# Second FFN of a decoder layer: products of mixed quads grouped by kind, five of eight quads mixed

## The chip, the cores and the metric

The kernel runs on one core of a Trainium2 chip. The metric is the device time of one execution in microseconds, as a median over runs. The engines that matter here are TensorE (PE in the profile; PEld is its weight loads), VectorE (DVE), ScalarE (ACT), and the queues of SyncE (SP) and GpSimd (POOL), which issue DMAs.

## The reference

One decoder layer over 272 positions (16 meta tokens and 256 of the sequence), model width 2048, all in fp32:

```
h += 0.5 * SwiGLU_1(RMSNorm(h))                 # 2048 -> 5632 -> 2048
z  = RMSNorm(h) @ W_in                          # q, k, v, indexer, conv, gates
h += W_out(sigmoid(ga) * attn(z) + sigmoid(gc) * conv(z))
h += 0.5 * SwiGLU_2(RMSNorm(h))                 # the second FFN
swiglu(x) = (silu(x @ w_gate) * (x @ w_up)) @ w_down
```

The change concerns the last line but one, the second FFN, where only the 256 positions of the output are computed: two halves of 128 tokens.

## The kernel before

**Products.** TensorE is fed with operands of the type fp32r. Every fp32 operand is split into a high part (ScalarE's copy to fp32r, `whi<-raw`, L175) and a low part (VectorE's subtraction, `wlo<-raw,whi`, L176). One product of a 128x128 block of tokens with a 128x512 block of weights is then three matmuls (`trio`, L407 to 410): high by high, high by low, low by high.

**The weight stream.** The class `Stream` brings in all weights in the order of use. A load is 1 MB at most (four weight blocks of 128x512), in one of four raw tiles (`raw` and `raws`), and SyncE's queue issues it. A *unit* is what one split makes ready, one or two blocks; its high and low parts lie in one of four pairs of buffers. Before TensorE's work of unit k is issued, the split of unit k+3 is (`AHEAD = 3`), so that it takes the buffers of unit k-1. The order on each engine is the order in which the program writes the instructions: `st.put(fn, slot)` puts a piece of other work `slot // 2` units on, an even slot before the split made there, an odd one behind it. The table `LAG` holds these slots.

**The second FFN.** It has two groups of 6 and 5 middle blocks of 512. A group has one *up stage* for each middle block f (gate and up together, 16 weight blocks deep), and then two *down parts* (d = 0 and d = 2), each for two groups of 512 output columns. Work in an up stage goes by *quads*: two weight blocks of depth (k) by two groups of 512 columns (gate and up), against two halves of tokens. An up stage has 8 quads, a down part 12 (first group) or 10 (second).

- A *plain* quad is 8 products on 4 weight blocks: two units of two blocks and four products.
- A *mixed* quad is Strassen-Winograd: 7 products P1 to P7. P1, P2 and P3 use the quad's own weight blocks, P4 to P7 sums of them. The sums of weights are made earlier by *jobs* (`job`, L554): a load of 1 MB on POOL's queue, four VectorE operations (L568, `made<-made`), and a store to scratch in DRAM. The sums of the inputs (`combos`) are five small VectorE operations (L702 to 706) and splits (ScalarE L688, VectorE L689).

Before, four of eight quads (1, 3, 5 and 6) are mixed in an up stage (one in the first), and 4, 4, 3 and 5 in the down parts: 57 in all. The units of a mixed quad, A, B, C and D, stand where the quad stands in the order, between plain ones (`order`, L89). P1, P5, P6 and P7 of all the mixed quads of a stage add up in banks of their own, and after the last mixed quad `spread` (L764) brings them together: one ScalarE copy (L767) and three VectorE adds (L768 to 770).

**At the end of an up stage** `gather` adds these sums to the other banks (VectorE L780 to 782, `few<-three,u`, `u<-one,u`, `u<-two,u`), two `silu` follow on ScalarE (L788), the product with up on VectorE (`times`, L794), then the transposition through DRAM (L637 and POOL's DMAs) and the split of the middle block (L812, L813). The last middle block of a group is turned on VectorE instead (sixteen transposes, L513), then split (ScalarE L464, VectorE L465, `mid<-mt`), since the down part reads it soon.

Of the jobs, 46 are done in the first FFN and 11 beside the output projection, before the second.

## Time and profile before

| what | value |
|---|---|
| median of 3 runs | 2109.67 us (2109.22 to 2110.75) |
| span of the profiled execution | 2106.9 us |
| PE, DVE, ACT busy | 2098.8, 1582.4, 1058.9 us |
| moved by DMA | 575.64 MB, mean 273 GB/s |
| second FFN in the profile | from about 1420 us to the end |

The profiled execution is one whose span is 2106.9 us; the median of the runs is 2.8 us above this span. A row of a timeline begins with its start and its length in us; a row of groups ends with busy us, mean ns of one, and the idle time before it with what ended it. A row "ACT whi L175 <- DVE wlo L176: 5.4, 5, 1.7" says who waited, for whom, how long in total, how often and the longest. Mean durations overlap a little from one VectorE instruction to the next, so that the distance of their starts (the pitch) is what counts in a sum.

### The profile page before, as it was taken

Reading aid. Unit: us, or ns where it says so; the run is one execution under the profiler, and the core shown is the slowest. Engines: PE = TensorE matmul, PEld = TensorE weight load, DVE = VectorE, ACT = ScalarE, POOL = GpSimd, SP = SyncE. Lnnn points to the kernel's source line nnn. Section 1 sums busy time; section 2 is a strip of 40 time slices with the busy share of each in tenths; the row PEclk is TensorE's granted clock in tenths of the full one; section 3 lists DMA queues with packets and bytes.
Section 4 is the critical chain, followed back from the end, with each engine's and each line's share of the span. In section 5 each row is a group of like instructions: output and inputs, shape, how many; then the busy total and the mean of one; then the engine's idle time right before and its main releaser. Section 6 shows DMA issues by size and latency. Waiting matters only on the chain.

```text
span 2106.9 us, 31863 instructions
## 1 busy us (share of the span) xinstructions
PE 2098.8 (100%) x12731; PEld 1889.9 (90%) x12731; DVE 1582.4 (75%) x2144; ACT 1058.9 (50%) x1342; POOL 106.0 (5%) x207
## 2 busy tenths in 40 slices
PE   9999999999999999999999999999999999999998
PEld 9999999999999999889988888888888888888887
DVE  7676766676776766578679678769788896878897
ACT  6444433344444445565444444456575565566654
POOL 0000000000000000000000000011000000000000
PEclk9999999999999999999999999999999999999999
DMA  7788888888888865445468886667988777799865
GB/s 265 260 320 327 324 315 322 311 337 310 322 313 325 328 224 177 164 159 181 152 216 329 323 301 223 219 233 255 314 314 300 281 268 247 282 306 319 306 250 207
DMA packets 85908, 575.64 MB, mean 273 GB/s; under 512 B 10112, under 2 KB 10880, under 8 KB 23808
## 3 DMA queue, kind: packets, MB, share of 16 engines
q1 hardware_dynamic: 64080, 438.34, 58.4%
q0 software_dynamic: 21104, 134.23, 17.1%
q8 instruction: 99, 1.62, 0.3%
q10 hardware_dynamic: 576, 1.05, 0.1%
q14 instruction: 49, 0.40, 0.1%
HBM read 504.90 MB, written 68.68 MB: 272 GB/s over the span
## 4 chain that ended last, share of the span: by engine, by line
PE 98%; DVE 1%; DMA 1%; issue 0%; ACT 0%; DVEq 0%; ACTq 0%
PE three L409 5%; PE three L408 5%; PE three L410 5%; PE pd L375 4%; PE pd L376 4%; PE pd L374 4%; PE pu L374 4%; PE pg L375 4%; PE pg L374 4%; PE pu L375 4%; PE pg L376 4%; PE pu L376 4%; PE pgt L402 3%; PE pgt L404 3%; PE pgt L403 3%; PE one L408 3%
## 5 line engine op out<-in xcount | busy, mean ns | idle before, releaser
L176 DVE TENSOR_TENSOR wlo<-raw,whi 128x1024 fp32r<-128x1024 f32 (+1 forms) x771 | 906.2, 1188 | 464.5 <-ACT whi L175 457.7
L175 ACT ACTIVATE whi<-raw 128x1024 fp32r<-128x1024 f32 (+1 forms) x771 | 786.4, 1030 | 883.4 <-PE pd L375 146.2
L375 PE MATMUL pd<-mid,whi 128*128 128x272 f32 x704 | 201.9, 287 | 0.0
L376 PE MATMUL pd<-mid,wlo 128*128 128x272 f32 x704 | 201.9, 287 | 0.0
L374 PE MATMUL pd<-mid,whi 128*128 128x272 f32 x704 | 201.9, 287 | 0.0
L374 PE MATMUL pu<-act,whi 128*128 128x272 f32 x672 | 192.8, 287 | 0.0
L376 PE MATMUL pu<-act,wlo 128*128 128x272 f32 x672 | 192.7, 287 | 0.0
L376 PE MATMUL pg<-act,wlo 128*128 128x272 f32 x672 | 192.7, 287 | 0.0
L375 PE MATMUL pg<-act,whi 128*128 128x272 f32 x672 | 192.7, 287 | 0.0
L375 PE MATMUL pu<-act,whi 128*128 128x272 f32 x672 | 192.7, 287 | 0.0
L374 PE MATMUL pg<-act,whi 128*128 128x272 f32 x672 | 192.7, 287 | 0.0
L568 DVE TENSOR_TENSOR made<-made 128x512 f32<-128x512 f32 x228 | 156.3, 685 | 0.0
L408 PE MATMUL three<-whi,act 128*128 128x512 f32 x352 | 137.2, 390 | 0.1
L409 PE MATMUL three<-wlo,act 128*128 128x512 f32 x352 | 137.0, 389 | 0.0
L410 PE MATMUL three<-whi,act 128*128 128x512 f32 x352 | 137.0, 389 | 0.0
L376 PEld LDWEIGHTS pd<-mid,wlo 128*128 128x128 f32 x704 | 132.7, 188 | 0.0
L374 PEld LDWEIGHTS pd<-mid,whi 128*128 128x128 f32 x704 | 132.7, 188 | 0.0
L375 PEld LDWEIGHTS pd<-mid,whi 128*128 128x128 f32 x704 | 132.7, 188 | 0.0
L176 DVE TENSOR_TENSOR wlo<-raws,whi 128x1024 fp32r<-128x1024 f32 x92 | 103.5, 1140 | 31.7 <-ACT whi L175 31.0
L374 PEld LDWEIGHTS pu<-act,whi 128*128 128x128 f32 x672 | 126.7, 188 | 0.0
L374 PEld LDWEIGHTS pg<-act,whi 128*128 128x128 f32 x672 | 126.7, 188 | 0.0
L376 PEld LDWEIGHTS pg<-act,wlo 128*128 128x128 f32 x672 | 126.6, 188 | 0.0
(381 smaller groups left out, 4482.7 us busy)
## 6 DMA issues: line engine op xcount, KB each, us to landing
raw<-in_wgu_dram SPq DMA_DIRECT2D x123, 1024.0 KB, 6.4
raw<-in_wd_dram SPq DMA_DIRECT2D x63, 1024.0 KB, 6.7
made<-in_wgu_dram POOLq DMA_DIRECT2D x41, 1024.0 KB, 10.6
made<-made POOLq DMA_DIRECT2D x41, 1024.0 KB, 6.5
raw<-made SPq DMA_DIRECT2D x31, 1024.0 KB, 6.1
raw<-in_wcv_dram SPq DMA_DIRECT2D x24, 1024.0 KB, 4.9
raw<-in_wgc_dram SPq DMA_DIRECT2D x24, 1024.0 KB, 5.1
raw<-in_wga_dram SPq DMA_DIRECT2D x24, 1024.0 KB, 5.4
```

Source lines behind the costliest of these rows:

```text
L175: nc.scalar.activation(hi[:, :n], raw, AF.Copy)
L176: nc.vector.tensor_sub(lo[:, :n], raw, hi[:, :n].bitcast(F32))
L374: nc.tensor.matmul(ps, whi, xhi, start=first, stop=False)
L375: nc.tensor.matmul(ps, whi, xlo, start=False, stop=False)
L376: nc.tensor.matmul(ps, wlo, xhi, start=False, stop=last)
L402: nc.tensor.matmul(ps, xhi, whi, start=k + i == 0, stop=False)
L403: nc.tensor.matmul(ps, xhi, wlo, start=False, stop=False)
L404: nc.tensor.matmul(ps, xlo, whi, start=False, stop=k + i == n - 1)
L408: nc.tensor.matmul(ps, x(0), w[0], start=first, stop=False)
L409: nc.tensor.matmul(ps, x(0), w[1], start=False, stop=False)
L410: nc.tensor.matmul(ps, x(1), w[0], start=False, stop=last)
L568: getattr(nc.vector, f"tensor_{op}")(to, a, b)
```

## The change

- In the up stages but the first, five quads of eight are mixed (0 to 4); in the first, none. In each of the four down parts four are: 66 in all.
- Products of the mixed quads are grouped by kind. An up stage runs (`mixed_first`): P1 of the five quads, P2, then P6, P7, P5 and the first P4, each unit two blocks of one kind in a row (13 units of two products), P3 with the plain quads behind, the rest of P4 between them. A down part runs (`plain_first`) 14 plain units in the first group's first part, 10 in the second group's (8 and 4 in the later parts), then the kinds.
- One bank takes several kinds in turn. After the last product of a kind ScalarE copies the bank out (`copy`, `u<-single` or `u<-double`); the adds of `spread` are gone, `gather` stays.
- Other work finds new slots: `times` one unit later, `turn_gated` in the calm units 16 to 18 of the next stage, the split of the middle block two stages later (units 14 and 15). The input sums of the down part stand at units 7, 9, 11, 13, their splits at 8, 10, 12, 14; a split is ScalarE's pieces and then VectorE's in one go. In the first up stage `silu` reads the banks directly.
- Jobs: 46 in the first FFN, 8 beside keys and queries (every 4 units), 12 beside the output projection. Each store goes to a tile where a quad's four sums lie apart, in pieces of 2 KB instead of 8 KB.
- The weights of the second FFN lie in DRAM in one stream in the order of use (`w2`), and once more for the jobs (`wj`). A load is of up to four blocks that follow each other in one of the two streams (own weights, sums). An up stage with mixed quads loads 47 blocks, where it was 44.

```diff
-MIXED = 1, 3, 5, 6
-FIRST_MIXED = 5,
+MIXED = 0, 1, 2, 3, 4
+DOWN_MIXED = (4, 4), (4, 4)
+EARLY_FROM = 2
+EARLY_EVERY = 4
+EARLY = 8
-DOWN_MIXED = {6: (6, 8, 9, 10), 5: (5, 6, 7)}
 LAG = dict(
-    spread=(0, 0, 1, 1), gather=(0, 0, 0), silu=(1, 1), times=(1,), turn=(1, 1), move=4, hi=(28, 33),
-    lo=(28, 33), last_times=(1,), last_turn=(5, 5, 8, 10), last_split=12, half=(3, 3), drain=(2, 4, 3),
+    silu=(1, 1), times=(3,), last_turn=(9, 9, 11, 13), last_split=14, drain=(0, 2, 4), below=7,
...
+def mixed_first(mixed, plain):
+    own = in_twos(of_kind("P1", mixed) + of_kind("P2", mixed))
+    made = in_twos(sum((of_kind(x, mixed) for x in ("P6", "P7", "P5", "P4")), []))
+    rest = in_twos(of_kind("P3", mixed) + sum(plain_pairs(plain), []))
+    early = -(-3 * len(mixed) // 2)
+    seq = [("h", x) for x in own] + [("m", x) for x in made[:early]]
+    made = made[early:]
+    for i, x in enumerate(rest):
+        seq.append(("h", x))
+        if i >= 2 and i % 2 == 0 and made:
+            seq.append(("m", made.pop(0)))
+    return seq
+def plain_first(mixed, plain, lead):
+    pairs = plain_pairs(plain)
+    seq = [("h", x) for x in pairs[:lead]]
+    pairs = pairs[lead:]
+    seq += [("h", x) for x in in_twos(of_kind("P1", mixed) + of_kind("P2", mixed))]
+    for name in ("P6", "P7", "P5", "P4"):
+        seq += [("m", x) for x in in_twos(of_kind(name, mixed))]
+        if name in ("P6", "P7"):
+            seq.append(("h", pairs.pop(0)))
+    seq += [("h", x) for x in in_twos(of_kind("P3", mixed))]
+    return seq + [("h", x) for x in pairs]
...
+            bank, xx = dict(
+                P1=lambda: (m, of(2 * i, 1)), P2=lambda: (c[1, 0], of(2 * i + 1, 1)), P3=lambda: (c[1, 1], s(i, 3)),
+                P4=lambda: (c[2, 0], of(2 * i + 1, 2)), P5=lambda: (m, s(i, 0)), P6=lambda: (m, s(i, 1)),
+                P7=lambda: (c[2, 0] if m is c[2, 1] else m, s(i, 2)),
+            )[name]()
...
-                plan.append((unit, i == max(mixed) and name == "D"))
+            for name in blocks:
+                if name in ends:
+                    ends[name]()
...
+                def split():
+                    for hi, lo, x in to:
+                        nc.scalar.activation(hi, x, AF.Copy)
+                    for hi, lo, x in to:
+                        nc.vector.tensor_sub(lo, x, hi.bitcast(F32))
...
-            def spread(m):
-                add = nc.vector.tensor_add
-                return (
-                    lambda: nc.scalar.activation(u[:, 1], m[1], AF.Copy),
-                    lambda: add(u[:, 0], m[6], u[:, 1]),
-                    lambda: add(u[:, 2], m[7], u[:, 0]),
-                    lambda: add(ends, m[5][:, None, :].to_broadcast([P, 2, 512]), u[:, 0::2]),
-                )
+            def copy(to, bank):
+                return lambda: st.put(lambda: nc.scalar.activation(u[:, to], bank, AF.Copy), 0)
...
+                    if mixed:
+                        copies = dict(P1=copy(1, m), P6=copy(2, m), P7=copy(3, c[2, 0]), P5=copy(0, m))
+                    quads(c, m, act_part, act_of, mixed, seq, copies)
+                    if mixed:
+                        put(gather(x, c), (0, 0, 0))
+                    put(silu(None if mixed else x), LAG["silu"])
...
+                        put(times(None if mixed else c), LAG["times"])
+                        put(turn_gated(box), (1, 3), calm)
...
+        for i, (src, to) in enumerate(made[JOBS : JOBS + EARLY]):
+            job(lambda i=i: early_home(i), src, to, st.at + EARLY_FROM + i * EARLY_EVERY, EARLY_EVERY, i < 3)
...
-    st.later(lambda: nc.gpsimd.dma_start(to, box["x"]), 1, at + every + 4)
+    st.later(
+        lambda: nc.gpsimd.dma_start(to, box["x"].rearrange("p (t c) -> p t c", t=4)), 1, at + every + 4
+    )
```

How VectorE's order at the boundary of two up stages changes is shown by its queue. Before, from the adds of `spread` (L769, L770) over `gather` (L780 to 782) to `times` (L794) and on:

```order
L769 TENSOR_TENSOR u<-two,u 128x512
L770 TENSOR_TENSOR u<-three,u 128x2x512
L176 TENSOR_TENSOR wlo<-raw,whi 128x1024
L780 TENSOR_TENSOR few<-three,u 128x1024
L781 TENSOR_TENSOR u<-one,u 128x512
L782 TENSOR_TENSOR u<-two,u 128x512
L176 TENSOR_TENSOR wlo<-raw,whi 128x512
L794 TENSOR_TENSOR few<-u,few 128x1024
L637 STREAM_TRANSPOSE mt<-few 128x4x4x32 x2
L176 TENSOR_TENSOR wlo<-raw,whi 128x1024 x4
```

Now (L238 is the low part of a weight split, L875 to 877 `gather`, L892 `times`):

```order
L238 TENSOR_TENSOR wlo<-raw,whi 128x1024 x3
L875 TENSOR_TENSOR few<-double_14357,u 128x1024
L876 TENSOR_TENSOR u<-single_14354,u 128x512
L877 TENSOR_TENSOR u<-single_14355,u 128x512
L238 TENSOR_TENSOR wlo<-raw,whi 128x1024
L238 TENSOR_TENSOR wlo<-raws,whi 128x1024
L892 TENSOR_TENSOR few<-u,few 128x1024
L238 TENSOR_TENSOR wlo<-raw,whi 128x1024 x6
L238 TENSOR_TENSOR wlo<-raws,whi 128x1024 x2
```

The adds of `spread` and the transposes (L637) are gone from this place. Between `gather` and `times` there are now two splits of two blocks in place of one of one block.

ScalarE at the same place, now (L237 is the high part of a weight split, L884 `silu`, L866 the copy of a bank):

```order
L237 ACTIVATE whi<-raw 128x1024 x2
L884 ACTIVATE few<-few,rcol 128x512 x2
L237 ACTIVATE whi<-raw 128x1024 x2
L866 ACTIVATE u<-single_14353 128x512
L237 ACTIVATE whi<-raw 128x1024
```

The first copy of a bank comes two splits behind the silus.

VectorE at the start of the second group's first down part, before (L513 the transposes of the last middle block, L465 its low part, L702 to 706 and L689 the sums of the inputs):

```order
L513 STREAM_TRANSPOSE mt<-few 32x2x4x32 x4
L176 TENSOR_TENSOR wlo<-raws,whi 128x1024
L465 TENSOR_TENSOR mid<-mt,mid 128x4x256
L702 TENSOR_TENSOR few<-mid 128x512
L703 TENSOR_TENSOR few<-few 128x128
L704 TENSOR_TENSOR few<-few 128x128
L705 TENSOR_TENSOR few<-few 128x128
L706 TENSOR_TENSOR few<-few 128x128
L176 TENSOR_TENSOR wlo<-raws,whi 128x1024
L176 TENSOR_TENSOR wlo<-raw,whi 128x1024
L689 TENSOR_TENSOR mid<-few,mid 128x128
```

Now (L590 the transposes, L542 the low part, L778 to 782 and L796 the sums):

```order
L590 STREAM_TRANSPOSE mt<-few 32x2x4x32 x4
L542 TENSOR_TENSOR mid<-mt,mid 128x4x256
L778 TENSOR_TENSOR few<-mid 128x512
L779 TENSOR_TENSOR few<-few 128x128
L780 TENSOR_TENSOR few<-few 128x128
L781 TENSOR_TENSOR few<-few 128x128
L782 TENSOR_TENSOR few<-few 128x128
L238 TENSOR_TENSOR wlo<-raws,whi 128x1024
L796 TENSOR_TENSOR mid<-few,mid 128x128
L796 TENSOR_TENSOR act<-few,act 128x3x128
```

The low part of the middle block now follows the last transpose directly, without a weight split between, and one weight split, not two, stands between a quad's sums and their low parts.

More of the change, by code (lines that the diff above doesn't have):

```diff
@@ L405, in tokens, with trio @@
             k += len(blocks)
[L407 to L412 removed]
+    def trio(ps, x, w, first, last, halting):
+        for i, (a, b) in enumerate(((0, 0), (0, 1), (1, 0))):
+            nc.tensor.matmul(
+                ps, x(a), w[b], start=first and i == 0, stop=last and i == 2, skip_group_check=halting
+            )
```

470 lines of the change are left out of this document (261 added, 209 removed).

## The prediction

> **What bounds the kernel now.** I read the page first, then the chain of waits, then the waits of TensorE, then timelines. The page:
>
> ```profile
> span 2106.9 us, 31863 instructions
> ...
> PE 2098.8 (100%) x12731; PEld 1889.9 (90%) x12731; DVE 1582.4 (75%) x2144; ACT 1058.9 (50%) x1342; POOL 106.0 (5%) x207
> ...
> DVE  7676766676776766578679678769788896878897
> ...
> PE 98%; DVE 1%; DMA 1%; issue 0%; ACT 0%; DVEq 0%; ACTq 0%
> ```
>
> TensorE is busy for the whole span and holds 98% of the chain that ends last. The time therefore falls by each matmul taken out, as long as nothing else makes TensorE wait. VectorE is the fullest of the others, and fullest in the last third of its slices, the second FFN. TensorE's waits in the second FFN are these two groups, 1.4 us together:
>
> ```profile
> PE three L409 <- DVE wlo L176: 1.1, 2, 0.8
> ...
> PE three L408 <- ACT whi L175: 0.3, 1, 0.3
> ```
>
> The pitch of a matmul of the second FFN, from the first and last of 33 in TensorE's timeline:
>
> ```profile
> 1445.68 0.39 PE L409 MATMUL three<-wlo,act 128*128 128x512 f32 x1
> ...
> 1452.94 0.39 PE L408 MATMUL three<-whi,act 128*128 128x512 f32 x1
> ```
>
> That is 7.26 / 32 = 0.227 us, so 0.68 us for a product of three. The window 1545 to 1586 (below) is busy for all of its 41.00 us: the products are the floor.
>
> **What the change takes away.** 57 mixed quads become 66, each with 7 products in place of 8: 9 x 3 = 27 matmuls fewer, 27 x 0.227 = **-6.1**. The two waits above belong to an order that is gone: **-1.4**. The adds that spread the sums leave VectorE, and ScalarE's copies between kinds come in. These are off TensorE's path: five products (3.4 us) run between a kind's end and the next kind's stop, against one copy of 0.58 us (L767 below). I cost both at nothing; without that cover each copy would be worth 0.58.
>
> **What it adds: units half as long.** A unit's split is one ScalarE copy (whi) and one VectorE subtraction (wlo). There are four buffers, so the split of unit k+3 starts when unit k-1 ends and has three units to be ready. Before, a mixed up stage opens with the two units of a plain quad, four products or 2.72 us each, and the split of its unit 3 has 2.72 + 2.72 + 1.36 = 6.8 us. Now it opens with thirteen units of two products (1.36 us): 4.08 us. The price of what has to fit in, by groups from 1463 to 2000 us (the first two after them are VectorE's timeline, with its starts one behind another):
>
> ```profile
> L176 DVE TENSOR_TENSOR wlo<-raw,whi 128x1024 fp32r<-128x1024 f32 x191 | 227.5, 1220 | 57.5 <-ACT whi L175 53.1
> L175 ACT ACTIVATE whi<-raw 128x1024 fp32r<-128x1024 f32 x192 | 200.1, 1058 | 133.0 <-PE three L410 108.4 <-PE one L410 14.4 <-DVE wlo L176 3.8
> ...
> L788 ACT ACTIVATE few<-few,rcol 128x512 f32<-128x512 f32 x22 | 14.7, 717 | 9.3 <-DVE few L780 9.3
> ...
> L794 DVE TENSOR_TENSOR few<-u,few 128x1024 f32<-128x1024 f32 x11 | 13.4, 1222 | 0.0
> ...
> L767 ACT ACTIVATE u<-three 128x512 f32<-128x512 f32 x12 | 6.9, 578 | 0.0
> ```
>
> ```profile
> 1503.17 1.22 DVE L780 TENSOR_TENSOR few<-three,u 128x1024 f32<-128x1024 f32 x1
> 1504.31 0.68 DVE L781 TENSOR_TENSOR u<-one,u 128x512 f32<-128x512 f32 x1
> 1504.91 0.68 DVE L782 TENSOR_TENSOR u<-two,u 128x512 f32<-128x512 f32 x1
> ...
> 1508.59 4.59 DVE L176 TENSOR_TENSOR wlo<-raw,whi 128x1024 fp32r<-128x1024 f32 x4
> ```
>
> ```profile
> 1504.43 1.34 ACT L788 ACTIVATE few<-few,rcol 128x512 f32<-128x512 f32 x2 [0.98 <-DVE few L780]
> ```
>
> A wlo holds VectorE for 1.14 us (1503.17 to 1504.31; four in 4.59), an add of half the width 0.60, and two silus hold ScalarE 1.34. In 1.36 us VectorE does one wlo and has 0.22 to spare. Let 0 be the first matmul of a mixed up stage after a mixed one. Unit 22 of the old stage ends at -1.36, and allowing 0.2 to the engine that waits, whi(2) runs from -1.14, wlo(2) from -0.05 to 1.09. Behind it in VectorE's queue stand the three gathers: 1.09, 2.22, 2.82. wlo(3) starts at 3.42 and is written at 4.64; unit 3 starts at 4.08 and its second matmul wants it at 4.31: **0.35** of waiting, with the hand-over. ScalarE's silus wait for the first gather (2.3 to 3.65), whi(4) behind them ends at 4.7, wlo(4) runs from 4.7 and is in time; then the product of gate and up (times) at 5.84 holds VectorE until 6.98, and wlo(5) is written at 8.20. Unit 5, pushed back by 0.35, wants it at 7.15 + 0.23 = 7.38: **0.84**. After this the 0.22 per unit suffices. So 1.2 per boundary, and there are eight: **+9.6**. Bounds: 0, if the hand-overs leave just 0.3 and the queue is less strict than I read it, and 2.4 each, were both waits doubled.
>
> The boundary after the first (unmixed) stage has silu reading the banks itself, and the table load stands in front of it:
>
> ```profile
> L788 ACT ACT_TABLE_LOAD x1 | 1.3, 1283 | 0.0
> ```
>
> 1.3 + 1.34 on ScalarE delay whi(4) past its unit: by the same sums 0.4 and then 1.0, **+1.4** (0 to 2.6).
>
> **The down parts.** At the start of the second group's first part stand the last middle block's transposes, its split and the sums of the four mixed quads. Before (VectorE, then ScalarE):
>
> ```profile
> 2003.64 3.57 DVE L513 STREAM_TRANSPOSE mt<-few 32x256 f32<-32x256 f32 x8
> ...
> 2014.54 1.22 DVE L465 TENSOR_TENSOR mid<-mt,mid 128x1024 fp32r<-128x1024 f32 x1
> 2015.67 0.69 DVE L702 TENSOR_TENSOR few<-mid 128x512 f32<-128x512 f32 x1
> ...
> 2017.33 1.22 DVE L176 TENSOR_TENSOR wlo<-raws,whi 128x1024 fp32r<-128x1024 f32 x1
> ...
> 2019.60 0.29 DVE L689 TENSOR_TENSOR mid<-few,mid 128x128 fp32r<-128x128 f32 x1
> ...
> 2020.27 0.69 DVE L176 TENSOR_TENSOR wlo<-raw,whi 128x512 fp32r<-128x512 f32 x1
> ```
>
> ```profile
> 2013.40 1.06 ACT L464 ACTIVATE mid<-mt 128x1024 fp32r<-128x1024 f32 x1 [2.83 <-DVE mt L513]
> ```
>
> Sixteen transposes are 2 x 3.57 = 7.1; a quad's sums 2015.67 to 2017.33, 1.66, and their splits 2019.60 to 2020.27, 0.67: 2.33 a quad, four 9.3. In the new order the split of the middle block follows the last transpose directly, so VectorE idles while ScalarE makes its high part, 1.1, and does its 1.14. With nine wlo (units 8 to 16) of 1.14, 10.3, VectorE needs 28.9 us from the first transpose to the sums that P6 of the fourth quad reads in unit 15. TensorE's work from the same point (2.4 into unit 4: whi and wlo of unit 7) is 5 x 2.72 + 0.3 to unit 10, then five units of 1.36 and one product: 21.6 at most. The difference, **+7.3**, comes in two places: unit 8 reads the last middle block (VectorE has it at 2.4 + 7.1 + 2.3 + 1.1 + 1.2 = 14.1, unit 8 would start at 10.9), about 3, and units 14 and 15, about 4. The bounds are 3 (unit 8 alone) and 10. The first group's part has fourteen plain units ahead where this has ten, so that its block is ready long before unit 12; only the tail of the sums falls among short units: **+0.9**. The last part's opening: **+0.4**.
>
> **Jobs beside keys and queries.** Four operations of this row for each of eight jobs, at a pitch of 0.60, are 19 us of VectorE:
>
> ```profile
> L568 DVE TENSOR_TENSOR made<-made 128x512 f32<-128x512 f32 x228 | 156.3, 685 | 0.0
> ```
>
> ```profile
> 815.00:860.00 45.00, 45.00 (x223) 38.05 (x222) 28.60 (x80) 24.52 (x44) 0.53 (x2) 1.00 0.55 187
> 860.00:910.00 50.00, 50.00 (x261) 39.84 (x260) 32.09 (x60) 25.97 (x29) 0.00 (x0) 1.00 0.44 149
> 1100.00:1240.00 140.00, 140.00 (x619) 116.02 (x618) 108.78 (x141) 60.50 (x61) 9.04 (x17) 1.00 0.86 322
> 1545.00:1586.00 41.00, 41.00 (x182) 33.92 (x182) 34.49 (x37) 25.86 (x29) 2.74 (x5) 1.00 0.90 319
> 1554.00:1568.00 14.00, 14.00 (x64) 11.59 (x63) 8.66 (x10) 7.54 (x9) 2.18 (x4) 1.00 0.99 316
> 1568.00:1581.00 13.00, 13.00 (x59) 10.74 (x58) 11.91 (x13) 10.08 (x12) 0.00 (x0) 1.00 0.93 356
> ```
>
> (Windows: length, busy time and count of PE, PEld, DVE, ACT, POOL, then granted clock, DMA share, GB/s.) From 815 to 910 VectorE is idle for 16.4 + 17.9 = 34 us and the DMA engines about half, so the jobs fit on the average. What they push is a chain of small operations that ends on VectorE and that TensorE reads. Its slack here is 2.6 us:
>
> ```profile
> 844.03 0.18 DVE L1000 TENSOR_TENSOR zk<-rot 128x32 f32<-128x32 f32 x1
> ```
>
> ```profile
> L1098 PEld LDWEIGHTS pkt<-ident,zk x4: 138/140/140, 846.8 to 847.3; 128*128 128x128 f32 x4
> ```
>
> An operation of 0.60 per unit pushes it by one or two of them. I take **+1.0** (0 to 3).
>
> **DMA.** A mixed up stage now loads 47 blocks of 0.262 MB where it was 44, and turns 1.05 MB: 13.4 MB in 40.1 us, 333 GB/s. In its thirteen short units it is 26 blocks in 17.7 us: 385 GB/s. With the engines full (share 0.99) the trace shows 316, at 0.93 it shows 356. At 356 the stage fits (37.6 us) and the run is short by 1.4 us, most of which the loads made ahead hold (four tiles of 1 MB); at 316 the whole stage is short by 2.2. I take the first, nearer row and 0.45 for each of nine stages: **+4** (0 to 20).
>
> The Trainium skill, "DMA: Bandwidth & Descriptors", section "Where 436 GB/s comes from", gives 435 GB/s for the ports of the 16 engines and about 358 GB/s for the HBM of one core, and has the latter bind between HBM and SBUF. By the 435 the run would need 15.7 us and this term would be nothing (sum 4 lower); by the 358 it is short, as I took it, and the windows, 316 to 356 when full or nearly, agree with that one.
>
> Job stores now go in pieces of 2 KB for 8 KB. The trace has stores of such rows, and none of them is slow for its size:
>
> ```profile
> made<-made POOLq DMA_DIRECT2D x41, 1024.0 KB, 6.5
> ...
> out_dram<-first SPq DMA_DIRECT2D x2, 256.0 KB, 2.2
> ```
>
> I take nothing; the bound is rival four.
>
> **Sum.** -6.1 - 1.4 + 9.6 + 1.4 + 7.3 + 0.9 + 0.4 + 1.0 + 4 = +17.1. Span 2106.9 + 17.1 = 2124.0; the median of the runs stands 2.8 above the span (2109.67), so **2127**.
>
> **Rivals.**
> 1. *The short units hold* (faster). If VectorE's work at a boundary is 1.2 us shorter than summed, wlo(3) and wlo(5) are in time; the margins are small against 8 us of queue. For it: TensorE waits for 1.4 us in the whole second FFN now. Against it: the same rows give waits as soon as three units are 4.08 long, and the down part would have to close 7 us as well. Left are -7.5: **2102**.
> 2. *Boundaries hold, the down part doesn't* (no change): -7.5 + 7.3 + 0.9 + 0.4 + 1.0 = +2.1, **2112**.
> 3. *DMA is the bound in the up stages*: 13.4 MB at 316 need 42.3 us, 2.2 more than TensorE's 40.1 for each of nine, 20 in place of 4: **2143**. For it, the share of 0.99 in the stage before; against it, the 356.
> 4. *Stores in 2 KB pieces take twice as long*: in the first FFN, where one job comes about each 15 us and the share is like the 0.86 shown, 3 us more per job make 1.06; some 4% of 690 us, **2155**.
>
> **Chances.** Forecast 0.70, rivals 0.05, 0.10, 0.12, 0.03. The range: down to 2 (2112) because DMA at 0, half the boundary waits and the down part's lower bound take about 13 off; up to rival 3: **2111 to 2145**; the forecast's own is 2116 to 2139. A measurement of this kernel tells 0.2%, 4.2 us, from no change: faster 0.05 (rival 1), same 0.10 (rival 2), slower 0.85.
>
> **What would show it.** In the changed profile: TensorE's waits for wlo appear in pairs at each mixed stage's start, near 0.35 and 0.84, at units 3 and 5; about 3 us in unit 8 and 4 in units 14 and 15 of the second group's first down part; ScalarE's waits for raw tiles grow in the short runs, the DMA share there being near 1; matmuls 27 fewer. It would be wrong if TensorE's waits in the up stages stay under 3 us in all, or if first FFN and keys change by more than 3.

## The result, and the profile after

The changed kernel takes **2135.2 us** (median of 4 runs, 2134.2 to 2135.9), the kernel before, run beside it, 2110.2 (4 runs, 2109.2 to 2112.2). The ratio is **1.0122**, 95% interval 1.0108 to 1.0136: 25.0 us slower, where the prediction had +17 (2127, range 2111 to 2145). The profiled execution of the changed kernel has a span of 2133.3, 26.4 above the one before; the sums below are made against these 26.4. The page after, the same lines as shown of before:

```profile
span 2133.3 us, 31823 instructions
...
PE 2111.1 (99%) x12704; PEld 1884.9 (88%) x12704; DVE 1584.8 (74%) x2134; ACT 1087.0 (51%) x1373; POOL 128.7 (6%) x225
...
DVE  7667666676676758877688688768787787787786
...
PE 74%; issue 18%; DMA 4%; DVE 2%; ACT 1%; POOL 1%; DVEq 0%; ACTq 0%; POOLq 0%
```

27 matmuls fewer (12731 to 12704), yet TensorE is recorded busy for 12.3 us more, and its share of the chain that ends last falls from 98% to 74%. VectorE does the same work in all as before (1582.4 and 1584.8): it isn't fuller, it is asked for its results sooner. TensorE's waits in the second FFN, two groups and 1.4 us before, are now five and 14.9 us:

```profile
PE single L470 <- DVE wlo L238: 7.1, 13, 1.7
PE single L470 <- ACT mid L541: 3.6, 1, 3.6
PE double L470 <- DVE wlo L238: 2.2, 10, 0.3
PE single L470 <- ACT act L794: 1.5, 1, 1.5
PE single L470 <- DVE act L796: 0.5, 1, 0.5
```

That leaves half of the loss to be found. From here a matmul's *lateness* is its start less the start of the one before and less the pitch of 0.227 (0.22677 unrounded, which over 3000 matmuls matters). Summed over the second FFN the lateness of all matmuls is 32.6 us, and was 2.8 before; less 27 x 0.227 = 6.1 the second FFN is 23.7 us longer. The other 2.7 lie before it.

**A boundary of two up stages.** TensorE's timeline, at units 3 and 5 of the third up stage, and VectorE's at the same place (L875 is `gather`'s first addition, L892 `times`):

```profile
1510.80 0.61 PE L470 MATMUL double<-whi,act 128*128 128x512 f32 x2
1511.62 0.50 PE L470 MATMUL double<-wlo,act 128*128 128x512 f32 x1 [0.20 <-DVE wlo L238]
1511.96 0.63 PE L470 MATMUL double<-whi,act 128*128 128x512 f32 x2
...
1514.27 0.39 PE L470 MATMUL single<-whi,comb 128*128 128x512 f32 x1
1515.14 0.50 PE L470 MATMUL single<-wlo,comb 128*128 128x512 f32 x1 [0.49 <-DVE wlo L238]
```

```profile
1508.03 1.22 DVE L875 TENSOR_TENSOR few<-double,u 128x1024 f32<-128x1024 f32 x1
...
1512.74 1.22 DVE L892 TENSOR_TENSOR few<-u,few 128x1024 f32<-128x1024 f32 x1
1513.87 2.35 DVE L238 TENSOR_TENSOR wlo<-raw,whi 128x1024 fp32r<-128x1024 f32 x2
```

The stage begins at 1506.95 (fifteen matmuls of P1 before the first of P2 at 1510.35), so `gather` starts at 1.08, where the sum had 1.09. The two matmuls are late by 1511.62 - 1511.03 - 0.227 = 0.37 (the second of the pair at 1510.80 starts 0.23 behind it) and by 1515.14 - 1514.27 - 0.227 = 0.65; the latter reads the first of the low parts that start at 1513.87, behind `times`, which is done 1.14 on. After each wait the next start is 0.34 on (1511.62 to 1511.96) and not 0.227: a wait costs 0.11 beyond itself. Together 1.24 for a boundary; the same pair stands at all eight.

**The second group's first down part** is late by 12.3 us in all:

```profile
2033.30 0.39 PE L470 MATMUL double<-whi,mid 128*128 128x512 f32 x1
2037.31 0.80 PE L470 MATMUL single<-whi,mid 128*128 128x512 f32 x1 [3.63 <-ACT mid L541]
...
2040.02 0.63 PE L470 MATMUL double<-whi,mid 128*128 128x512 f32 x1
2040.45 0.63 PE L470 MATMUL single<-whi,mid 128*128 128x512 f32 x1
...
2044.13 0.40 PE L470 MATMUL double<-whi,mid 128*128 128x512 f32 x1
...
2053.72 0.50 PE L470 MATMUL single<-wlo,act 128*128 128x512 f32 x1 [0.34 <-DVE wlo L238]
2054.06 0.40 PE L470 MATMUL single<-whi,act 128*128 128x512 f32 x1
2055.94 0.50 PE L470 MATMUL single<-whi,act 128*128 128x512 f32 x1 [1.48 <-ACT act L794]
2056.27 0.40 PE L470 MATMUL single<-wlo,act 128*128 128x512 f32 x1
2057.18 0.50 PE L470 MATMUL single<-whi,act 128*128 128x512 f32 x1 [0.52 <-DVE act L796]
...
2061.16 0.40 PE L470 MATMUL double<-whi,mid 128*128 128x512 f32 x1
```

```profile
2040.00:2044.00 4.00, 4.00 (x11) 3.11 (x10) 3.96 (x7) 2.18 (x3) 0.00 (x0) 0.51 0.02 4
```

(A window, its columns as in the prediction.) The waits are 3.78 in unit 8 and 0.50, 1.65 and 0.68 in units 14 and 15: 6.6, where the sum had 7. What it didn't have is what stands between: after the long wait matmuls start 0.43 apart (the first three 0.60 to 0.66), at a granted clock of 0.51, until 2044.13. The 15 steps from 2037.31 to there take 6.82 for 3.40; the 10 from 2057.18 to 2061.16 take 3.98 for 2.27. **The half clock costs 3.4 + 1.7 = 5.1 us**, counted as busy time.

### The profile page after: what moved, and what is told of

It is laid out like the page before. It is cut to its first block, busy times and chain, and to the rows that moved or that the text cites. A ratio compares the mean times of both kernels' runs of the same rounds, so it can differ in the third digit from the quotient of the medians.

```text
span 2133.3 us, 31823 instructions
## 1 busy us (share of the span) xinstructions
PE 2111.1 (99%) x12704; PEld 1884.9 (88%) x12704; DVE 1584.8 (74%) x2134; ACT 1087.0 (51%) x1373; POOL 128.7 (6%) x225
## 4 chain that ended last, share of the span: by engine, by line
PE 74%; issue 18%; DMA 4%; DVE 2%; ACT 1%; POOL 1%; DVEq 0%; ACTq 0%; POOLq 0%
PE single L470 5%; PE pd L435 4%; PE pd L437 4%; PE pd L436 4%; PE pg L437 4%; PE pu L437 4%; PE pg L436 4%; PE pu L436 4%; PE pu L435 4%; PE pg L435 4%; PE double L470 3%; DMA hold<-mt 3%; PE pgt L463 3%; PE pgt L465 3%; PE pgt L464 3%
## 5 line engine op out<-in xcount | busy, mean ns | idle before, releaser
L238 DVE TENSOR_TENSOR wlo<-raw,whi 128x1024 fp32r<-128x1024 f32 (+1 forms) x762 | 916.1, 1212 | 470.8 <-ACT whi L237 464.3
L237 ACT ACTIVATE whi<-raw 128x1024 fp32r<-128x1024 f32 (+1 forms) x762 | 792.2, 1049 | 849.3 <-PE pd L436 144.4
L470 PE MATMUL single<-whi,act 128*128 128x512 f32 x552 | 195.0, 390 | 2.0 <-ACT act L794 1.5
L645 DVE TENSOR_TENSOR made<-made 128x512 f32<-128x512 f32 x264 | 180.6, 684 | 2.7 <-DMA made<-in_wj_dram 2.7
L470 PE MATMUL double<-whi,act 128*128 128x512 f32 x504 | 180.4, 390 | 0.0
L238 DVE TENSOR_TENSOR wlo<-raws,whi 128x1024 fp32r<-128x1024 f32 (+1 forms) x91 | 108.6, 1207 | 33.8 <-ACT whi L237 33.0
L437 PEld LDWEIGHTS pu<-act,wlo 128*128 128x128 f32 x672 | 126.6, 188 | 0.0
L436 PEld LDWEIGHTS pg<-act,whi 128*128 128x128 f32 x672 | 126.6, 188 | 0.0
L435 PEld LDWEIGHTS pg<-act,whi 128*128 128x128 f32 x672 | 126.6, 188 | 0.0
```

The costliest lines, as they stand in the source:

```text
L237: nc.scalar.activation(hi[:, :n], raw, AF.Copy)
L238: nc.vector.tensor_sub(lo[:, :n], raw, hi[:, :n].bitcast(F32))
L435: nc.tensor.matmul(ps, whi, xhi, start=first, stop=False)
L436: nc.tensor.matmul(ps, whi, xlo, start=False, stop=False)
L437: nc.tensor.matmul(ps, wlo, xhi, start=False, stop=last)
L470: nc.tensor.matmul(ps, x(a), w[b], start=first and i == 0, stop=last and i == 2, skip_group_check=halting)
```

## The experiments

Theory: the loss is the waits of units that come too fast for VectorE (boundaries, down part), with the loads behind them. Rivals: the loads themselves, the jobs beside keys and queries, the clock. Each difference below is of a median to that of the kernel before in the same series, which lies between 2107.98 and 2110.21; the changed kernel has +25.0. Where two medians differ by 2 us or less, only the traces can say more.

**1 (e1). The operands' place.** The second FFN's first matmul starts at 1421.60 (before: 1418.94): 2.7 us are lost ahead of it, and no wait shows there but at the keys (0.65). Two groups of products are slower there, and read stationary operands (`c`, `ms`) that start 128 bytes past a multiple of 256 in the changed layout, and at a multiple before. Paddings put these and `over` (another stationary operand, of the second FFN) back on multiples:

```diff
+    const.tile([P, 8], F32, name="pad")
-    TABLES = 3 * ROPE + BOTH + 2 * P + 88
+    TABLES = 3 * ROPE + BOTH + 2 * P + 80
...
+            if i in (0, 2):
+                mp.tile([P, 32], F32, name=f"pad{i}")
```

> The changed kernel with three pads, so that the tiles c, ms and over begin at multiples of 256 bytes within a partition again (they begin 128, 128 and 224 bytes past one; in the kernel before, the tiles in their place, cs and ms, were aligned). Theory (the start of the stationary operand sets the matmul's pitch): the pitch of pbr<-c falls from 0.232 to 0.227 us (192 matmuls, -1.1), of po<-ms likewise in half of its 384 (-1.1), of the products on over (90, -0.6); the first matmul of the second FFN starts 2.0 us earlier, the span falls from 2133.3 to about 2130.6, the median from 2135.2 to about 2132.5. Rival (the slower pitch comes from what runs beside, the jobs' DMAs and VectorE operations): the pitch stays, 2135.2 within 1.

Measured: 2131.99, ratio 1.0111 (1.0096 to 1.0126), +22.7: 2.2 less. Groups by line, of the changed kernel and then of this one:

```profile
L463 PE MATMUL pbr<-whi,c 128*128 128x512 f32 x64 | 25.3, 395 | 0.0
L463 PE MATMUL po<-whi,ms 128*128 128x512 f32 x128 | 50.2, 392 | 0.0
```

```profile
L464 PE MATMUL pbr<-whi,c 128*128 128x512 f32 x64 | 24.9, 389 | 0.0
L464 PE MATMUL po<-whi,ms 128*128 128x512 f32 x128 | 49.8, 389 | 0.0
```

The same matmuls, the same data, 6 and 3 ns shorter: 192 x 6 and 384 x 3 ns are 2.3 us. The second FFN starts at 1419.42. The interval of the difference overlaps that of the changed kernel, and the profiled execution is the slowest of the four; the rows are what shows it. From the 7000th matmul to the second FFN all seven traces with these tiles off a multiple take 518.93 to 518.95 us, the six others 516.76 to 516.90.

**2 (e5). The jobs beside keys and queries** taken out, and all done in the first FFN instead (54, every 4 units):

```diff
-JOBS_EVERY = 5
-JOBS = 46
+JOBS_EVERY = 4
+JOBS = 54
...
-EARLY = 8
+EARLY = 0
```

> The changed kernel without jobs beside keys and queries: 54 jobs in the first FFN, one every 4 units instead of every 5, 12 late ones as before. Theory (the early jobs cost TensorE 0.65 us beside keys and queries, the jobs in the first FFN nothing): the keys' first products come 0.6 us earlier, the rest stays; median 2135.2 - 0.6, about 2134.6. Rival (25% more jobs per time take the first FFN's DMA to its bound, share 0.86 to about 0.95, with waits for raw tiles): the first FFN grows by 2 to 8 us, median 2137 to 2143.

Measured: 2133.21, ratio 1.012 (1.0105 to 1.0135), +25.2. The medians show no difference. But the edit does two things: without the early jobs' tiles, `c` and the first of `ms` begin at multiples of 256 here as well, with no padding, and their products last 389 to 390 ns. The second FFN starts at 1419.48, and the profiled span is 2130.8, 2.5 below that of the changed kernel. So the time doesn't tell what the jobs cost. The traces do: from the 6500th matmul to the 7000th, beside keys and queries, TensorE takes 94.40 before, 94.74 in the changed kernel and 94.40 here. The jobs push by 0.34 there, and by 0.33 to 1.92 in the nine other traces that have them. The queries' first transposition stands at 872.19 before, 872.84 in the changed kernel and 872.73 here; the rest of that 0.65, and all of what is left here, has come up by the 500th matmul, at 67.34, 67.60 and 67.86.

**3 (e2). The boundary's work spread.** `gather`, the silus and `times` of an up stage leave VectorE in pieces, with room between:

```diff
-                        put(gather(x, c), (0, 0, 0))
+                        put(gather(x, c), (0, 5, 9) if f < n - 1 else (0, 0, 0))
...
-                        put(times(None if mixed else c), LAG["times"])
+                        put(times(None if mixed else c, True), (13, 17) if mixed else (13,))
```

> The changed kernel with the work at the boundary of two up stages spread over VectorE's queue: the three gathers in units 0, 2 and 4, the silus behind the split made in unit 1, the product of gate and up in two halves in units 6 and 8 of the next stage. The work is the same. Theory (VectorE's queue of gathers and product in units 0 to 2 is what makes TensorE wait in units 3 and 5): these waits vanish at eight boundaries, 8 x 1.24 (0.37 + 0.65 and 0.11 behind each) = -9.9, and a third of the first boundary's 1.5; a mixed up stage takes 40.8 where it took 42.0; median 2135.2 - 10.4 = about 2125. Rival (the short units are limited by something else, ScalarE, the buffers or the loads): the waits come back a few units later, the stages stay above 41.7, median above 2132.

Measured: 2129.13, ratio 1.0097 (1.0082 to 1.0112), +19.9: 5.1 less, half of what the waits were. The pairs at units 3 and 5 are gone, and others have come, behind ScalarE's wait for a load. ScalarE's timeline and a window round it:

```profile
1936.62 2.01 ACT L237 ACTIVATE whi<-raw 128x1024 fp32r<-128x1024 f32 x2 [2.56 <-DMA raw<-sums_up]
```

```profile
1928.00:1940.00 12.00, 10.26 (x41) 7.21 (x40) 8.40 (x10) 7.24 (x9) 0.00 (x0) 1.00 1.00 350
```

The DMA engines are full there. The boundary's waits had given the loads time.

**4 (e8). The same with half the bytes of sums.** To tell whether loads are what took the other half: each load of sums in an up stage takes half of its columns, and the units read them twice (the other half of the sums is left out of the result).

```diff
+                if len(seq) == 24 and n == RAW:
+                    src, n = src[:, : RAW // 2], RAW // 2
...
-                a += len(seq[i][1])
+                a = (a + len(seq[i][1])) % (n // HALF)
```

> The kernel with the spread boundary work (e2), in which each full load of sums of weights in an up stage brings two blocks instead of four, and both units that use it read these two: about 2.6 MB of 13.4 less in each of nine stages (and a result that is not the layer's). Everything else is as in that run. Theory (half of the gain from the spread boundary was given back to loads that come late): the waits behind loads, some 7 us in that run's second FFN, go; median 2129.1 - 6, about 2123. Rival (what is left is ScalarE's and VectorE's queue): within 1.5 us of 2129.1.

Measured: 2119.47, ratio 1.0051 (1.0036 to 1.0066), +11.5: 8.4 less than in 3. An up stage with mixed quads, behind another, is late by 0.2 us now (0.5 to 3.6 in 3). So the loads it was. What is left above the kernel before is mostly the down part, which this kernel leaves as it is.

**5 (e12). Half the bytes, the changed kernel otherwise as it is.** The edit is that of 4, without that of 3:

```diff
+                if len(seq) == 24 and n == RAW:
+                    src, n = src[:, : RAW // 2], RAW // 2
```

> The changed kernel in which each full load of sums of weights in an up stage brings two blocks instead of four, and both units that use it read these two (2.6 MB of 13.4 less a stage, and a result that is not the layer's); nothing else is changed. Theory (in the changed kernel itself the loads are nearly in time, since the waits at the boundaries give them a head start): the waits behind loads seen in its trace, about 1 us, go, and with them little else: median 2135.2 - 1 to 2, about 2133.5. Rival (the loads cost as much as the prediction gave them or more): 4 to 10 us less, 2125 to 2131.

Measured: 2129.81, ratio 1.0097 (1.0083 to 1.0111), +20.5: 4.5 less. I had expected 2 at most and the rival 4 or more: the rival was right. Loads cost the changed kernel some 4 to 5 us even behind its boundary waits; about 2.4 of them in the up stages by the timeline (17.0 us of lateness there to 14.6). The second group's first down part is late by 9.9 instead of 12.3: the wait of unit 8 is 2.94 instead of 3.78, and the half clock behind it lasts 3.41 us instead of 6.83, which depends on where the wait falls (experiment 7).

**6 (e3). The down part's start repaired.** The last middle block is split two units later; in the second group the units of P1 and P2 are drawn ahead of the plain quad that reads this block first; and the sums of three quads are made in the last up stage:

```diff
-    silu=(1, 1), times=(3,), last_turn=(9, 9, 11, 13), last_split=14, drain=(0, 2, 4), below=7,
+    silu=(1, 1), times=(3,), last_turn=(9, 9, 11, 13), last_split=18, drain=(0, 2, 4), below=7,
...
-    seq = [("h", x) for x in pairs[:lead]]
-    pairs = pairs[lead:]
+    seq = [("h", x) for x in pairs[: lead - behind]]
     seq += [("h", x) for x in in_twos(of_kind("P1", mixed) + of_kind("P2", mixed))]
+    seq += [("h", x) for x in pairs[lead - behind : lead]]
...
+                    if f == n - 1:
+                        home = down_home(g)
+                        for i in range(3):
+                            at = 19 + i
+                            put_combos(middle, i, home(i), (g, i), 2 * at, 2 * at + 2)
```

> The changed kernel with the input sums of three of the four mixed quads of a down part made in the calm end of the last up stage instead of the down part's units 7 to 12, the split of the last middle block two units later, and in the second group's first part the kinds P1 and P2 ahead of the last block's plain quad. Theory (VectorE and the in-order ScalarE have too much in the first units of a down part, and TensorE's pace falls with the wait): TensorE's waits of 6.8 us in the second group's part fall to about 2, the stretches in which a matmul takes 0.43 us instead of 0.227 (4.6 us lost) go, the first group's 2.2 us go: 13.7 - 2 = -11.7, median about 2123.5. Rival (the last up stages have no room for the sums, so that the waits move ahead): the last up stage of each group grows by 2 to 4 us, median 2128 to 2131.

Measured: 2127.58 (2126.0, 2126.2, 2129.0, and one of 2147.7 that makes the interval wide), ratio 1.0119 (1.0069 to 1.0169). The profiled execution's span is 2123.9, 9.4 below that of the changed kernel. By the timeline the two first down parts together are late by 2.1 instead of 15.1, while the up stages' lateness grows from 17.0 to 19.5. Why the block was late shows in ScalarE's waits and VectorE's timeline of the changed kernel:

```profile
ACT mid L911 <- DMA mt<-hold: 4.7, 1, 4.7
```

```profile
2021.48 0.69 DVE L912 TENSOR_TENSOR mid<-mt,mid 128x512 fp32r<-128x512 f32 x1 [2.95 <-ACT mid L911]
...
2026.45 3.57 DVE L590 STREAM_TRANSPOSE mt<-few 32x256 f32<-32x256 f32 x8
...
2037.29 1.23 DVE L542 TENSOR_TENSOR mid<-mt,mid 128x1024 fp32r<-128x1024 f32 x1 [1.12 <-ACT mid L541]
```

The split of the block *before* the last (L911, L912), which the change moved, stands in both queues ahead of the transposes and waits for its DMA. VectorE stands still for 2.95 us and ScalarE for 4.7. This is not the whole of it: in experiment 9, with the same down parts, that split waits for nothing, and unit 8 still waits 2.42 us where it was 3.78; in experiment 10, where it waits 4.5 and the stage ahead ends as in 9, unit 8 waits 3.26. So some 0.8 to 1.4 are this split's, and 2.4 are there without it. Here that split stands where it did, but waits only 0.46 for its DMA (why was not followed), and the last block's split, two units later, finds the transposes done:

```profile
2035.31 1.06 ACT L542 ACTIVATE mid<-mt 128x1024 fp32r<-128x1024 f32 x1
...
2041.65 0.50 PE L471 MATMUL single<-wlo,mid 128*128 128x512 f32 x1 [1.82 <-DVE wlo L239]
```

One wait of 2.0 us is left of 6.6, no matmul runs at the half clock, and the part is late by 2.1 instead of 12.3.

**7 (e4). Waits put into the kernel before.** Is the half clock a matter of the wait alone? One subtraction in each group's last down part is done seven and six times over:

```diff
-            nc.vector.tensor_sub(lo[:, :n], raw, hi[:, :n].bitcast(F32))
+            for _ in range(1 + self.again.get(self.n_split, 0)):
+                nc.vector.tensor_sub(lo[:, :n], raw, hi[:, :n].bitcast(F32))
...
+                    if d:
+                        st.again[st.n_split + 2] = (6, 5)[g]
```

> The kernel before with one weight split's VectorE subtraction done 7 times instead of once in the first group's last down part, and 6 times in the second group's last down part (the same result written again). It makes TensorE wait there for about 3 us and 2 us, with plain units around and nothing else changed. Theory 1 (after a wait of some us TensorE's granted clock falls for a while): behind the 3 us wait some 10 to 17 matmuls take 0.43 us, as in the changed kernel at 2038 to 2044, the granted clock of those 10 us is below 0.9, and the place costs 3 + 2 to 3.5 us. Theory 2 (the slow pace in the changed kernel comes from what ran beside it there): the pitch is 0.227 directly behind the waits, the two places cost 5 to 6 us in all.

Measured in one execution: 2116.8, 7.6 above the kernel before. TensorE's timeline at the two places:

```profile
1742.66 0.39 PE L410 MATMUL one<-whi,mid 128*128 128x512 f32 x1
1746.35 0.80 PE L411 MATMUL one<-wlo,mid 128*128 128x512 f32 x1 [3.31 <-DVE wlo L178]
...
1749.81 0.40 PE L410 MATMUL three<-whi,mid 128*128 128x512 f32 x1
...
2067.65 0.39 PE L410 MATMUL one<-whi,mid 128*128 128x512 f32 x1
2070.04 0.50 PE L411 MATMUL one<-wlo,mid 128*128 128x512 f32 x1 [2.00 <-DVE wlo L178]
...
2074.03 0.40 PE L412 MATMUL three<-whi,mid 128*128 128x512 f32 x1
```

Waits of 3.46 and 2.16 us bring the half clock, in a kernel that has none of the change: the 8 steps from 1746.35 to 1749.81 take 3.46 for 1.81, the 10 from 2070.04 to 2074.03 take 3.99 for 2.27. A wait of some 2 to 3.5 us costs 1.7 on top. It doesn't always: in experiment 1 TensorE waits 2.9 us and goes on at full clock (timeline):

```profile
1700.86 0.50 PE L471 MATMUL single<-whi,mid 128*128 128x512 f32 x1
1703.96 0.50 PE L471 MATMUL single<-wlo,mid 128*128 128x512 f32 x1 [2.60 <-DVE wlo L238]
```

So the wait's length alone doesn't decide. The records of the granted clock in the traces say what else does. The stretches of half clock last 3.41 or 6.83 us, and within a trace all their edges while TensorE works lie on one grid of 3.413 us. In the changed kernel they begin at 2037.10 and 2057.58, six steps apart; here at 1746.24 and 2070.51, 95 steps apart. Between two points of this grid in experiment 1, and at the same place in experiment 10, where a shorter wait (2.41 us) does bring the half clock, the windows are (third number from the right: the granted clock):

```profile
1698.80:1702.21 3.41, 2.55 (x11) 1.53 (x9) 2.25 (x4) 2.14 (x3) 0.00 (x0) 1.00 0.62 257
1702.21:1705.62 3.41, 1.66 (x7) 1.39 (x8) 3.41 (x7) 2.60 (x4) 0.00 (x0) 1.00 0.01 2
```

```profile
1699.79:1703.20 3.41, 1.16 (x6) 0.62 (x4) 3.34 (x8) 1.72 (x4) 0.00 (x0) 1.00 0.18 72
1703.20:1706.61 3.41, 3.41 (x8) 2.76 (x9) 3.34 (x9) 1.57 (x3) 0.00 (x0) 0.50 0.23 38
```

The grid cuts the wait of experiment 1 in two, and leaves the other whole. Over the thirteen traces, from 1080 us (output projection and second FFN) to the last matmul, all 20 windows at full clock whose waits, each counted within the window alone, add up to 2.18 us or more were followed by half clock, and none of those with 1.97 or less. Where the grid lies differs from trace to trace, so one and the same wait can cost 1.7 more in one execution and nothing in the next.

**8 (e6). All repairs together, five quads mixed**: the edits of 1, 3 and 6 (of 6 with the transposes and the last block's split one unit earlier), and besides the table load of the first boundary made ahead, and the middle block's turning and splits moved behind the short units:

```diff
+                    if not mixed:
+                        st.put(lambda: nc.scalar.activation(rcol[:, 1, 8:9], known("rcol", rcol[:, 0, :1]), AF.Silu), 29)
...
-                        calm = nxt - 8
+                        calm = nxt - (8 if f == n - 2 else 5)
...
-                        at = nxt + (2 if f == n - 2 else length(("up", g, f + 2)) - 10)
+                        at = nxt + (2 if f == n - 2 else length(("up", g, f + 2)) - (10 if f == n - 3 else 7))
```

> The changed kernel with all that the first runs pointed to: the aligned tiles, the spread boundary work, the early input sums and the split of the last middle block at a later place, the transposes one unit earlier, the middle blocks' splits in units 17 and 18 instead of 14 and 15 (the turn behind them), and one silu in the calm of the first up stage, so that its table is loaded ahead. Theory (the costs are separate and add up): -2.2, -5.1 and -8 as measured one by one, -1.6 for the middle blocks' splits, -0.5 for the table: 2135.2 - 17.4, about 2118, still above the kernel before. Rival (with VectorE out of the way the loads of the short units are the bound, as the second run hints, and what is taken from one place comes back there): 2122 or more.

Measured: 2129.93, ratio 1.0103 (1.0088 to 1.0118), +22.0. I had expected +8. The down part is late by 0.7, no boundary shows; seven of the up stages are late by 2.0 to 6.3 each, in ScalarE's waits for loads and TensorE's behind them (in the two latest with a stretch of half clock besides):

```profile
1560.05 2.00 ACT L238 ACTIVATE whi<-raw 128x1024 fp32r<-128x1024 f32 x2 [5.01 <-DMA raw<-sums_up]
```

```profile
1561.16 0.51 PE L472 MATMUL double<-whi,over 128*128 128x512 f32 x1 [1.81 <-ACT whi L238]
```

The waits that were repaired had been the time in which the loads caught up. With five of eight mixed the loads are next in line, right behind VectorE.

**9 (e9). Four quads mixed, not five**, nothing else.

```diff
-MIXED = 0, 1, 2, 3, 4
+MIXED = 0, 1, 2, 3
```

> The changed kernel with four of eight quads mixed instead of five (56 mixed quads, one less than before the change), grouped by kind as in the changed kernel. Ten products more: 30 x 0.227 = +6.8. Theory (the loss comes with the grouping by kind, whatever the number of mixed quads: the boundary's 1.24 us per stage, the down parts' 13.7 and the tiles' 3 stay, and only the load waits of about 1 us and a job's worth of small things go): 2135.2 + 6.8 - 1 = about 2141, and so 31 us above the kernel before at nearly the same number of products. Rival (the fifth quad makes the run of short units too long, and its load and queue waits are the loss): the boundary and load waits fall by more than half, median 2131 or less.

Measured: 2127.98, ratio 1.0095 (1.0078 to 1.0112), +20.0, with 30 matmuls (6.8 us) *more* than the changed kernel. My theory had it at 2141: it fell. TensorE's waits behind loads are gone, as one would expect, but so is most of the boundary's. A stage with four mixed quads ends with a whole unit, one with five (17 blocks in the run of P3 and plain quads) with a single block, half a unit. VectorE's and TensorE's timelines:

```profile
1507.73 1.23 DVE L875 TENSOR_TENSOR few<-double,u 128x1024 f32<-128x1024 f32 x1 [0.40 <-PE double L470]
```

```profile
1514.86 0.50 PE L470 MATMUL single<-wlo,comb 128*128 128x512 f32 x1
```

The stage begins at 1507.53 (the sixth unit at 1514.33 less five of 1.36), so `gather` starts at 0.20, where it was 1.08; of 1.24 per boundary 0.42 is left, and none of it in unit 3. The second group's first down part, which the edit doesn't touch, is late by 8.0 instead of 12.3, with unit 8's shorter wait (experiment 6) and 3.41 us of half clock.

**10 (e10). Five quads mixed, the single block elsewhere** (right behind P3, so that the stage ends with whole units) tells that apart from the number of quads:

```diff
-    rest = in_twos(of_kind("P3", mixed) + sum(plain_pairs(plain), []))
+    blocks = of_kind("P3", mixed) + sum(plain_pairs(plain), [])
+    n = len(mixed) + len(mixed) % 2
+    rest = in_twos(blocks[:n]) + [blocks[n : n + 1]] * (len(blocks) % 2) + in_twos(blocks[n + len(blocks) % 2 :])
```

> The changed kernel with one unit moved: the 17 blocks behind the made ones (P3 of five quads and twelve plain ones) leave one block alone, which the changed kernel puts at the end of the up stage; here it stands behind P3, so that the stage ends with three whole plain units. Theory (VectorE's lead into the next stage is set by the stage's last unit: with four products there, as with four mixed quads, the split of unit 2 is done 1.36 us earlier): the boundary's 1.24 us shrink to the 0.42 seen with four mixed quads, 8 x 0.82 = -6.5, median about 2128.7 if the loads keep up. Rival (the loads set the pace of the short units, so that what is saved at the boundary is waited for a few units later, as when the boundary work was spread): the wait for wlo in unit 5 goes, waits behind loads come, less than 3.5 us are saved, median 2131.5 or more.

Measured: 2127.52, ratio 1.0083 (1.0067 to 1.0098), +18.2: 6.8 less, 6.5 expected. The boundary has one wait of 0.31 with its 0.11, like 9. The place of one unit in the order was two thirds of the boundary's price.

**11 (e11). Four quads mixed, all repairs**, the best that the runs pointed to. Against 8:

```diff
-MIXED = 0, 1, 2, 3, 4
+MIXED = 0, 1, 2, 3
...
-                        put(gather(x, c), (0, 5, 9) if f < n - 1 else (0, 0, 0))
+                        put(gather(x, c), (0, 0, 0))
...
-                        put(times(None if mixed else c, True), (13, 17) if mixed else (13,))
+                        put(times(None if mixed else c, True), (9, 13) if mixed else (13,))
```

> Four of eight quads mixed, grouped by kind, with the aligned tiles, the early input sums and later split in the down parts, the product of gate and up in two halves in units 4 and 6, the middle blocks' split behind the short units, and the silu table loaded ahead. Theory (with 44 blocks a stage the loads keep up, so here the repairs do add up): 2128.0 - 2.2 (tiles) - 7.5 (down parts) - 3.4 (boundaries) - 1.3 (first boundary) = about 2113.5, some 4 us above the kernel before. Rival (the loads bind here too): 2118 or more.

Measured: 2109.36 (11 runs, 2108.8 to 2111.0) beside 2109.33 for the kernel before: ratio 1.0002, 0.9993 to 1.0010; I had expected 2113.5. The profiled span is 2107.0, 0.1 above that of the kernel before. TensorE's waits in the second FFN, the whole list:

```profile
PE single L472 <- DVE wlo L239: 0.5, 2, 0.3
```

The new order can be had without waits, and then it is worth what its products are: 3 matmuls more than before, and the same time. A version that beats both wasn't found. Five mixed quads, all repairs and halved loads together were not run: halved loads leave work out, so it would be no version of the layer. Nor was the unit order of experiment 10 together with the repaired down part.

## Why the prediction was right, and where it was off

Direction and mechanism held: TensorE waits for VectorE's low parts in pairs at the boundaries and again at the second group's down part, and the loads run short behind them. The sum was +17.1 against the 26.4 of the spans. Term by term, predicted and measured:

| term | predicted | measured |
|---|---|---|
| 27 products fewer | -6.1 | -6.1 |
| the old order's waits | -1.4 | -2.8 |
| eight boundaries | +9.6 | +9.9 |
| the boundary after the unmixed stage | +1.4 | +1.5 |
| second group's first down part | +7.3 | +12.3 |
| first group's first down part | +0.9 | +2.8 |
| the last part's opening | +0.4 | +0.5 |
| keys and queries (jobs) | +1.0 | +0.65 (0.34 of it the jobs) |
| loads in the short runs | +4 | +2.8 |
| the rest of the up stages' lateness | - | +2.9 |
| the operands' place before the second FFN | - | +2.0 |
| sum | +17.1 | +26.4 |

**Boundaries.** The walk through VectorE's queue came out nearly to the number, with 0.37 for 0.35 and 0.65 for 0.84, and the 0.11 after each wait, which the sum didn't have, making up the difference by luck. That it rested on the stage's last unit being a single block was in the sum (unit 22 at -1.36), but not seen as something that could be changed for nothing; experiments 9 and 10 are what that would have shown.

**The down part** is the step that failed most: *about 3 in unit 8 and 4 in units 14 and 15* were 3.8 and 2.8, so the waits were sized nearly right, in part by luck. The split of the block before the last, moved "two stages later" by the change, wasn't followed into this part; by experiments 9 and 10 it is some 0.8 to 1.4 of the 3.8. Nothing stood in the sum for what a wait does to the matmuls behind it: the half clock is 5.1 of the 12.3, and takes the term beyond its own upper bound of 10. No row of the trace before has a wait of over about 1 us in the second FFN, so it couldn't be read there. The Trainium skill, "TensorE: Matmul & The Clock Gate", Part 1, "What's actually happening", says that the gate halves TensorE's clock after an idle window of about 3.4 us, and that the windows run freely. The stretches of 3.41 and 6.83 us on one grid are one and two such windows, and starts 0.43 apart are half speed, which agrees; that some 2.2 us without work within a window are enough (experiment 7) goes beyond the page's length of gap.

**First group's down part**: the same ScalarE queue; L541 stands there for 6.5 us behind the transposes and ahead of a weight's high part, and unit 10 waits 1.9. The split of the block before the last adds to it: where it waits for nothing (experiments 5 and 9), L541 stands for 5.5 us, unit 10 waits 0.8, and the part is late by 1.7 instead of 2.8. I had this block "ready long before unit 12", which it was; what was late was the unit behind it in the queue.

**Loads.** The term's size is right by experiment 5 (4.5 in all) and by short waits in the up stages (2.8), but part of it lies in the down parts. (It counted nine up stages; ten are mixed, but the one behind a down part is late by only 0.2.) The rate I took, 316 to 356, is too low for a short run. The changed kernel's windows:

```profile
1515.00:1527.00 12.00, 11.86 (x52) 9.64 (x53) 10.25 (x10) 8.75 (x10) 0.00 (x0) 1.00 0.99 381
1852.00:1866.00 14.00, 13.51 (x59) 10.92 (x59) 12.24 (x11) 10.16 (x13) 0.00 (x0) 1.00 0.98 389
```

At 385 the short run of 17.7 us would just fit, and by itself leave no term. The loads cost all the same; that a late one can't be made up while the DMA engines are full (share 0.98 to 0.99) is my reading, and no run shows it apart. The Trainium skill, "DMA: Bandwidth & Descriptors", "Where 436 GB/s comes from", has about 358 GB/s bind between HBM and SBUF; 381 and 389 over 12 and 14 us lie above it. The 350 of experiment 3, at share 1.00, doesn't: the rate isn't one number here.

**Rivals.** *The short units hold* and *boundaries hold, the down part doesn't* fell to the pairs of waits in the timeline. *DMA is the bound in the up stages* was wrong of this kernel (2143 for 2135) but right one step on: with the boundaries repaired it is the bound, and takes the gain (experiments 3, 4 and 8). *Stores in 2 KB pieces* fell: from 100 to 200 us, in the first FFN, TensorE runs 813 matmuls in both kernels.

**Jobs.** The 0.65 by which the queries' first transposition is later lies inside the term's bounds, but only 0.34 of it is the jobs'; the rest has come up in the first 70 us of the program. In other traces with the same jobs the push is up to 1.92, so the +1.0 was a fair size.

**What no term had**: the pitch of products with operands off a multiple of 256 bytes (2.0), and 2.9 of small lateness in the up stages: some 5 ns for a dozen matmuls after each wait, and `over`'s products at the slower pitch. The chances (0.85 slower) and the range fitted. The forecast's own range ended at 2139 and holds the 2135, though the down part, at 12.3, lies outside its own bounds of 3 to 10: the room came from other terms, the loads' 0 to 20 above all. That is luck.

## What to carry to other kernels

Grouping work into shorter units saves nothing unless each engine in the chain, and the loads, keep up unit for unit: walk the queue of the fullest engine through the *first* units after a boundary, and after repairing one limit ask for the next (here VectorE first, then the loads). The last unit of a stage decides how much of the boundary's work is done before the next begins, so end a stage on a full unit. Follow every moved instruction into the stage in which it now lands, and reckon that a TensorE wait of over 2 us may bring 1.7 us of half clock besides, twice that behind one of nearly 4.

## What the runs showed of the hardware that I had not expected

- A wait costs TensorE 0.11 us beyond itself (the next start 0.34 on), and some 5 ns for each of a dozen matmuls behind it.
- The granted clock falls to half for 3.41 or 6.83 us, on a grid of 3.413 us whose place differs from trace to trace. In thirteen traces, from 1080 us on, every window of it with waits of 2.18 us or more in it was followed by half clock (20 windows), and none with 1.97 or less: a wait of 2.41 us within one window brought it (experiment 10), one of 2.88 cut in two by the grid didn't (experiment 1), and 1.65 and 0.68 within one window did (changed kernel). What makes it last for two windows instead of one stays open.
- A 128x512 product with a stationary operand that starts 128 bytes past a multiple of 256 lasts 395 ns where an aligned one lasts 389, by pitch about 6 ns in 227. A padding of 128 bytes per partition ahead of the tiles takes it away.
- 16 DMA engines moved 381 to 389 GB/s over 12 to 14 us on one core, and 350 in another kernel at the same full share.
